# Sums of w_down beside the output projection, moving tiles on GpSimd's queue, and later products with ones, in a hybrid SSD and ConvFFN decoder step

## The chip, the cores and the metric

The kernel runs on one core of a Trainium2 chip. The metric is the device time of one execution in microseconds (us), lower is better. Before the change three runs gave 1511.21, 1513.53 and 1514.72 us, with a median of 1513.53.

The engines are named as in the profile: PE is the matrix engine (TensorE) and PEld its loading of weights, DVE is VectorE, ACT is ScalarE, POOL is GpSimd. SP is SyncE, which here only starts transfers. Transfers can be started by SP, ACT and POOL; each starts its own in the order in which the program puts them, and an instruction that waits holds back all that stands behind it on the same engine.

## The reference

One layer of a decoder is computed for 1032 tokens (a prompt of 1024 and 8 single-token samples), all in float32:

```python
x = x + jnp.concatenate([y_ssd, y_pool], axis=-1) @ w_out      # 2048 -> 1024
hn = rmsnorm(x, norm2_w)
u = hn @ w_up                                                  # 1024 -> 2 x 2816
u, ffn_new = causal_dwconv(u, ffn_buf, ffn_conv_w, ffn_conv_b)
gate, val = jnp.split(u, 2, axis=-1)
x = x + (jax.nn.silu(gate) * val) @ w_down                     # 2816 -> 1024
y = rmsnorm(x, final_norm_w)
```

What comes before it (input projection, short convolution, chunked SSD scan, windowed means) gives `y_ssd` and `y_pool`; the change doesn't touch it.

## The kernel before, in words

Everything is held with channels on the 128 partitions and the 1032 tokens along the free dimension. To keep the accuracy of float32, each operand of a matmul is split into a high part, rounded by ACT (L137 for weights, L207 for moving tiles), and a low part, the difference made by DVE (L138, L208). Each product of two tiles is then three matmuls (high x high, high x low, low x high).

**Output projection** (`w_out`, L834). It runs in three parts over the contraction, 6, 6 and 4 tiles of 128. In each of the first two parts a loop goes over the 8 output tiles n: `load_tile` loads the weights `wout` in two pieces on SP's queue (L127, into four buffers called `raw`), 54 matmuls of 344 columns are made (L156 to L158), and DVE adds the result to the residual `x2[n]` (L855). The third part (`w_out_end`, L877) runs by halves of the tokens, stores x2 to DRAM as `x2d` (L893, SP), makes the squares for the RMSNorm and scales x2 by it (L915).

**Up-projection** (`up_pair`, L1013, 22 pairs). `w_up` and `w_down` are multiplied by Strassen's scheme in Winograd's form: seven products p1 to p7 of half-sized blocks in place of eight. `moving` (L925) makes the sums of blocks of the normalised x2 and their splits, once; these are the moving operands of all 22 pairs. `up_weights` (L975) makes the sums of blocks of the weights by accumulating transfers: SP loads a block into a buffer `s` (L985), and GpSimd's queue adds another to it during a transfer (L987). The chain is p5 from two blocks, p6 from one block plus p5, p3 from one plus p6, and p7 from two. Each product of a pair is 24 matmuls of 258 columns (`blocks`, L990, matmul L1008), 168 in a pair. Behind a pair come the convolution (L1053, L1055), SiLU and the product with the value (L1065); every second pair `spill` (L1079) makes the block sums of the activations and ACT's queue stores them to DRAM as `td`.

**Sums of w_down** (`down_sums`, L1095). The down projection's seven products need four sums of blocks of `w_down` (p5, p7, p6, p3). The contraction is cut in three pieces s (`PIECES`: 4, 4 and 3 tiles), and the output in four column pairs m. For each of the twelve (m, s), SP loads four blocks `ds` (L1104), GpSimd makes four additions (`mix`, L1107) and GpSimd's queue stores each result to DRAM as `sd` (L1109). `phase_ffn` (L1310) calls it once behind each pair from the third on (L1326); the blocks lie in five buffers of the pool `sums`, where the seven buffers `s` lie as well.

**Down projection** (`down`, L1159). The products come in the order p1, p2, p5, p6, p7, p4, p3. `down_ops` (L1117) loads the 11 moving tiles of a product from `td` (L1124, SP's queue) and splits them; `down_weights` (L1131) loads a piece of weights, from `w_down` or from `sd` (L1142, SP's queue); `piece` (L1145) makes 12 or 9 matmuls (L1154), so that a product is 264. `sink` adds the results to the residual, which `load_x2` (L1167) brings back from `x2d` in front of p2; the additions that read only SBUF are GpSimd's (L1182), those that read PSUM are DVE's. `square` (L1208) collects squares for the last RMSNorm, added by GpSimd (L1216).

**Last block.** p3 runs by quarters q of the tokens, and in each over the four column pairs. Beside its matmuls stand products with ones, which sum squares over the partitions: of `ssq[1]` ahead of the first column pair (L1259), and of the pair's own squares behind each pair (L1272). After the first column pair `norm_half` (L1294) makes the norm of the first half of the tokens: two products with ones (L1301), eight multiplications on DVE (L1305) and eight stores of `yT` on SP's queue (L1308). At the end of each quarter the norm is applied (L1280, L1288) and stored (L1286, L1292).

A scheduler orders the instructions of each engine when the program is built, by its own estimate of times and by the buffers; it doesn't keep the order of the source. `issue_after` (`behind`, L172) is the means to force one instruction behind another.

## Time and profile before

| | |
|---|---|
| median of three runs | 1513.53 us |
| the profiled execution | 1515.61 us, of which its span 1513.8 us |
| mean granted clock of PE | 0.961 |
| output projection, matmuls of the first two parts | about 556 to 692 us of the span |
| up-projection, first to last matmul | 747.7 to 1243.1 us |
| down projection, first to last matmul | 1250.2 to 1504.9 us |
| moved by transfers | 227.53 MB, 150 GB/s on average |

The profile is that of one execution. Its page gives the busy time of each engine, the share that each line has in the chain of work that ended last, and groups of instructions by line. The trace behind it can also be asked for stretches of time, for the waits between engines (who waited for whom, total, times, longest), and for the order of events on one engine. A busy time of PE counts each matmul from start to end; matmuls overlap, so the pace is read from a count of matmuls in a stretch.

### The profile page before, as it was taken

The numbers are of one execution on the slowest core, as the hardware profiler recorded it, in microseconds if no ns is written. First come the engines' busy times: TensorE is split into PE (matmuls) and PEld (weight loads), VectorE is DVE, ScalarE is ACT, GpSimd is POOL, SyncE is SP. The second block draws the span as 40 slices with busy tenths as digits, with TensorE's granted clock in tenths as the row PEclk, the third lists the DMA queues.
The fourth block names the chain that finished last, engine by engine and source line by source line (L and its number), as shares of the span: only waits on it lengthen the run. The fifth ranks groups of instructions, "written<-read, shape, count | busy, mean of one in ns | idle before, by whom it ended". The sixth has DMA issues, their size and how long they took to land.

```text
span 1513.8 us, 26445 instructions
## 1 busy us (share of the span) xinstructions
PE 1411.6 (93%) x10312; PEld 1334.4 (88%) x10312; DVE 998.7 (66%) x1442; ACT 669.8 (44%) x1220; POOL 542.0 (36%) x536
## 2 busy tenths in 40 slices
PE   8999999798999999999839989999999989999977
PEld 6889878776699999999839989999999989999966
DVE  6484786699953482524778978877777765667532
ACT  6246443255245451313435444545555554454422
POOL 5153677768621100001386766322222101003310
PEclk9999999999899999999959999999999999999989
DMA  6031333333311142124559999977777766765431
GB/s 231 8 94 56 110 118 115 121 109 126 110 46 37 46 149 66 47 56 135 180 146 251 306 295 273 265 191 184 195 182 189 186 204 231 246 222 184 133 113 57
DMA packets 132120, 227.53 MB, mean 150 GB/s; under 512 B 27852, under 2 KB 45084, under 8 KB 131996
## 3 DMA queue, kind: packets, MB, share of 16 engines
q1 hardware_dynamic: 102012, 170.31, 35.3%
q0 software_dynamic: 16256, 34.61, 11.3%
q10 hardware_dynamic: 13728, 20.93, 4.2%
q8 instruction: 81, 1.33, 0.4%
q14 instruction: 43, 0.35, 0.1%
HBM read 169.11 MB, written 45.15 MB: 142 GB/s over the span
## 4 chain that ended last, share of the span: by engine, by line
PE 68%; DMA 10%; DVE 10%; POOL 6%; issue 4%; ACT 2%; SPq 1%; DVEq 0%; ACTq 0%; POOLq 0%
PE g L1008 22%; PE g L1154 10%; PE g L157 10%; PE g L156 10%; PE g L158 10%; DMA g<-td 3%; DVE wop L138 2%; POOL ds L1107 2%; DMA s<-wup 2%; PE pY L579 2%; PE pY L583 1%; DMA ds<-wdn 1%; DMA mix<-acd 1%; PE pT L534 1%; PE pT L532 1%
## 5 line engine op out<-in xcount | busy, mean ns | idle before, releaser
L1008 PE MATMUL g<-op,wop 128*128 128x258 f32 x3696 | 454.1, 286 | 41.4 <-ACT wop L137 23.0
L1008 PEld LDWEIGHTS g<-op,wop 128*128 128x128 f32 x3696 | 451.2, 192 | 44.2 <-ACT wop L137 33.0
L1154 PE MATMUL g<-op,wop 128*128 128x258 f32 x1848 | 233.6, 288 | 12.9 <-ACT op L207 8.4
L1154 PEld LDWEIGHTS g<-op,wop 128*128 128x128 f32 x1848 | 228.9, 193 | 17.2 <-ACT op L207 9.4
L156 PE MATMUL g<-hh,wop 128*128 128x344 f32 x696 | 229.1, 329 | 2.9 <-ACT u L464 2.8
L138 DVE TENSOR_TENSOR wop<-raw,wop 128x512 fp32r<-128x512 f32 (+1 forms) x186 | 142.9, 774 | 130.1 <-ACT wop L137 129.3
L158 PE MATMUL g<-hh,wop 128*128 128x344 f32 x696 | 227.1, 326 | 0.0
L157 PE MATMUL g<-hl,wop 128*128 128x344 f32 x696 | 226.5, 325 | 0.0
L137 ACT ACTIVATE wop<-raw 128x512 fp32r<-128x512 f32 (+1 forms) x208 | 125.5, 607 | 227.8 <-PE g L158 137.2
L156 PEld LDWEIGHTS g<-hh,wop 128*128 128x128 f32 x696 | 134.0, 193 | 4.7 <-ACT u L464 3.5
L158 PEld LDWEIGHTS g<-hh,wop 128*128 128x128 f32 x696 | 133.7, 192 | 1.2 <-issue 1.1
L157 PEld LDWEIGHTS g<-hl,wop 128*128 128x128 f32 x696 | 134.0, 193 | 0.5 <-issue 0.5
L1055 DVE SCALAR_TENSOR_TENSOR acc<-u,cst,acc 128x1048 f32<-128x1048 f32 x88 | 124.5, 1415 | 10.7 <-ACT acc L1053 9.3
L137 ACT ACTIVATE wop<-s 128x512 fp32r<-128x512 f32 (+1 forms) x136 | 82.4, 614 | 97.2 <-PE g L1008 39.1
L138 DVE TENSOR_TENSOR wop<-s,wop 128x512 fp32r<-128x512 f32 (+1 forms) x136 | 105.7, 783 | 29.0 <-ACT wop L137 28.1
L987 POOL DMA_DIRECT2D s<-s x44 | 40.0, 909 | 200.5 <-DMA s<-wup 88.6
L1040 ACT ACTIVATE u<-g 128x258 f32<-128x258 f32 (+2 forms) x220 | 69.1, 338 | 77.4 <-PE g L1008 66.1
L1107 POOL TENSOR_TENSOR ds<-ds,ds 128x512 f32<-128x512 f32 (+1 forms) x48 | 87.6, 1835 | 28.4 <-DMA ds<-wdn 28.1
L1043 DVE TENSOR_TENSOR u<-u,g 128x258 f32<-128x258 f32 (+2 forms) x176 | 57.4, 352 | 58.7 <-PE g L1008 57.1
L479 DVE SCALAR_TENSOR_TENSOR xs<-u,cst,xs 128x1056 f32<-128x1056 f32 x48 | 78.3, 1647 | 23.9 <-ACT xs L477 23.6
L158 PE MATMUL g<-yh,wop 128*128 128x344 f32 x288 | 91.8, 320 | 0.0
L157 PE MATMUL g<-yl,wop 128*128 128x344 f32 x288 | 91.8, 320 | 0.0
(262 smaller groups left out, 2313.9 us busy)
## 6 DMA issues: line engine op xcount, KB each, us to landing
s<-wup SPq DMA_DIRECT2D x88, 256.0 KB, 4.7
g<-td SPq DMA_DIRECT2D x77, 258.0 KB, 3.7
raw<-wup SPq DMA_DIRECT2D x66, 256.0 KB, 5.0
raw<-win SPq DMA_DIRECT2D x58, 256.0 KB, 2.6
mix<-acd SPq DMA_DIRECT2D x16, 768.0 KB, 6.0
td<-acc ACTq DMA_DIRECT2D x22, 516.0 KB, 5.7
s<-wup POOLq DMA_DIRECT2D x44, 256.0 KB, 6.1
s<-s POOLq DMA_DIRECT2D x44, 256.0 KB, 4.6
```

What stands on the lines that cost most here:

```text
L137: self.nc.scalar.activation(hi, raw[:, :w], AF.Copy)
L138: lo_eng.tensor_tensor(out=lo, in0=raw[:, :w], in1=hi.bitcast(F32), op=ALU.subtract)
L156: nc.tensor.matmul(ps[:, :n], wh, xh[:, sl], start=(first and k == 0), stop=False)
L157: nc.tensor.matmul(ps[:, :n], wh, xl[:, sl], start=False, stop=False)
L158: nc.tensor.matmul(ps[:, :n], wl, xh[:, sl], start=False, stop=(final and k == last))
L479: nc.vector.scalar_tensor_tensor(out=out, in0=u[:, k : k + SW], scalar=self.c("cw", 4 * ct + k), in1=out, op0=ALU.mult, op1=ALU.add)
L1008: nc.tensor.matmul(out, a, b, start=(p in OPENS and j == 1), stop=(j == 12), skip_group_check=True)
L1040: a = nc.scalar.activation(out, ps[:, s], AF.Copy, scale=-1.0 if p in ("p5", "p4") else 1.0)
L1043: nc.vector.tensor_tensor(out=out, in0=out, in1=ps[:, s], op=op)
L1055: nc.vector.scalar_tensor_tensor(out=acc, in0=u[:, k : k + FW], scalar=self.c("fw", 3 * n + k), in1=acc, op0=ALU.mult, op1=ALU.add)
L1107: nc.gpsimd.tensor_tensor(out=out, in0=in0, in1=in1, op=op)
L1154: nc.tensor.matmul(out, a, b, start=(s == 0 and i == 0 and j == 0), stop=(s == len(PIECES) - 1 and i == nk - 1 and j == 2),)
```

## The change

Four things are edited.

1. `down_sums` is called in the output projection, once at each output tile of the first two parts until the twelve are done. Its blocks take buffers that the pooling groups leave behind (`v`, `mh`, `ml`, `sa`, `sb`, 4 KB a partition each), two sets by turns, and the five buffers `ds` are gone.
2. The loads of moving tiles (`td`), the loads of `x2d` and the stores of `norm_half` are started by GpSimd in place of SP. The loads of `x2d` come behind the tiles of p1.
3. The 32 additions of `sink` that read only SBUF go from GpSimd to DVE, and squares get two buffers of their own in place of buffers `s`.
4. In the last block the products with ones wait for one column pair more, by a list `held` and by `behind`; `norm_half` follows the second column pair.

```diff
+        self.sums = {}
+        todo = [(m, s) for s in range(len(PIECES)) for m in range(KT // 2)]
...
             for n in range(KT):
+                if todo:
+                    self.down_sums(len(todo), *todo.pop(0))
...
-    def down_sums(self, m, s):
+    def down_sums(self, i, m, s):
...
+        mk = lambda tag, bufs=1: self.ph.tile([P, 2, 512], F32, tag=tag, name=self.nm("ds"), bufs=bufs)
+        x, y, z = mk("v", 2), mk(("mh", "ml")[i % 2]), mk(("sa", "sb")[i % 2])
+        blk = {"11": x[:, 0, :w], "12": x[:, 1, :w], "21": y[:, 0, :w], "22": y[:, 1, :w]}
...
-                self.nc.sync.dma_start(st[:, j], self.td[i + j][ROW[p]])
+                self.loaded = self.nc.gpsimd.dma_start(st[:, j], self.td[i + j][ROW[p]]).ins
...
-                nc.sync.dma_start(t, self.x2d[n])
+                with self.behind(self.loaded):
+                    nc.gpsimd.dma_start(t, self.x2d[n])
...
-                add(nc.gpsimd, block(0, 0), u)
+                add(nc.vector, block(0, 0), u)
...
-        mksq = lambda: self.raw(True)
+        mksq = lambda: self.ph.tile([P, TH], F32, tag="sq", name=self.nm("sq"), bufs=2)
...
-            if p == "p2":
+            if p == "p1":
                 load_x2()
...
-            nc.tensor.matmul(pb[:, :TQ], self.ones, ssq[1][:, part], start=True, stop=False)
+            held = [ssq[1][:, part]]
+
+            def ones(stop=False):
+
+                with self.behind(self.pe):
+                    nc.tensor.matmul(pb[:, :TQ], self.ones, held.pop(0), start=(m == 1), stop=stop)
...
-                nc.tensor.matmul(pb[:, :TQ], self.ones, sq, start=False, stop=(m == NM - 1))
-                if q == 0 and m == 0:
-                    self.norm_half(x2, 0, ssq[0], r_of(0))
+                held.append(sq)
+                if m:
+                    ones()
+                if q == 0 and m == 1:
+                    with self.behind(self.pe):
+                        self.norm_half(x2, 0, ssq[0], r_of(0))
+            ones()
+            ones(True)
...
-            nc.sync.dma_start(d["yT"][:, n, cols], x)
+            nc.gpsimd.dma_start(d["yT"][:, n, cols], x)
...
-                    if j >= 2 and todo:
-                        self.down_sums(*todo.pop(0))
```

The built programs show what the scheduler makes of it. First GpSimd at the opening of the up-projection. A row has the line, the operation and what it writes and reads: `s` are sums of up weights, `wup` their blocks, `ds` and `sd` the sums of w_down, `u` the tiles of the convolution. Before:

```order
L987 DMA s_6955<-wup 128x512
L987 DMA s_6963<-wup 128x512
L987 DMA s_7209<-wup 128x512
L987 DMA s_6958<-s_6955 128x512
L987 DMA s_7217<-wup 128x512
L1107 TENSOR_TENSOR ds_7718<-ds_7716,ds_7718 128x512
L1109 DMA sd_7726<-ds_7718 128x512
L1107 TENSOR_TENSOR ds_7716<-ds_7720,ds_7716 128x512
L1107 TENSOR_TENSOR ds_7724<-ds_7718,ds_7720 128x512
L987 DMA s_7212<-s_7209 128x512
L1109 DMA sd_7729<-ds_7716 128x512
L987 DMA s_6966<-s_6958 128x512
```

With the change (its L992 is L987 of before):

```order
L992 DMA s_7183<-wup 128x512
L992 DMA s_7191<-wup 128x512
L992 DMA s_7437<-wup 128x512
L992 DMA s_7186<-s_7183 128x512
L992 DMA s_7445<-wup 128x512
L992 DMA s_7440<-s_7437 128x512
L992 DMA s_7194<-s_7186 128x512
L1026 MEMSET u_7175 128x2
L1027 COPY u_7175<-fst_7173 128x24
```

The load of p3's sum (`s_6966` before, `s_7194` now) stood behind three additions and two stores of `down_sums`, and now stands behind other accumulating loads alone.

Second, SP in the first two parts of the output projection. Before, weights follow weights:

```order
L127 DMA raw_5393<-wout 128x384
L127 DMA raw_5398<-wout 128x384
L127 DMA raw_5463<-wout 128x384
L127 DMA raw_5468<-wout 128x384
L127 DMA raw_5533<-wout 128x384
```

With the change (`ds` are blocks of w_down, x2 marks two equal rows):

```order
L127 DMA raw_5596<-wout 128x384
L127 DMA raw_5601<-wout 128x384
L1110 DMA ds_5222<-wdn 128x512 x2
L127 DMA raw_5685<-wout 128x384
L127 DMA raw_5690<-wout 128x384
L1110 DMA ds_5221<-wdn 128x512 x2
L1110 DMA ds_5311<-wdn 128x512 x2
L127 DMA raw_5798<-wout 128x384
L127 DMA raw_5803<-wout 128x384
```

`ds_5222` and `ds_5221` belong to the third sum and take the buffers of the first; the weights behind them wait on the queue until the first sum's additions and stores have let those buffers go.

Third, SP at the last block. Before (`s` from `sd` are weights of p3, `yT` from `x` the stores of `norm_half`):

```order
L1142 DMA s_15377<-sd_7735 128x512
L1142 DMA s_15394<-sd_8853 128x512
L1142 DMA s_15411<-sd_9971 128x384
L1308 DMA yT<-x_13330 128x516
...
L1308 DMA yT<-x_13344 128x516
L1142 DMA s_15455<-sd_8015 128x512
L1142 DMA s_15472<-sd_9133 128x512
```

With the change (`raw` from `wdn` are weights of p4, the product before):

```order
L1148 DMA s_15352<-sd_5060 128x512
L1148 DMA s_15369<-sd_5416 128x512
L1148 DMA s_15386<-sd_5796 128x384
L1148 DMA s_15405<-sd_5149 128x512
L1148 DMA s_15422<-sd_5505 128x512
L1148 DMA s_15439<-sd_5885 128x384
L1148 DMA s_15483<-sd_5238 128x512
L1148 DMA raw_15046<-wdn 128x512
L1148 DMA raw_15075<-wdn 128x384
L1148 DMA raw_15110<-wdn 128x512
L1148 DMA raw_15139<-wdn 128x512
```

The stores of `norm_half` are off this queue, and seven of the twelve weights of p3 (the `s` of these rows) stand ahead of the last weights of p4.

More of the change, by code (lines that the diff above doesn't have):

```diff
@@ L1099, in down_sums @@
         w = nk * P
-        blk = {}
-        for k, i, e in (("21", 1, 0), ("22", 1, 1), ("11", 0, 0), ("12", 0, 1)):
-            blk[k] = self.spool.tile([P, 512], F32, tag="ds", name=self.nm("ds"), bufs=5)[:, :w]
+        mk = lambda tag, bufs=1: self.ph.tile([P, 2, 512], F32, tag=tag, name=self.nm("ds"), bufs=bufs)
+        x, y, z = mk("v", 2), mk(("mh", "ml")[i % 2]), mk(("sa", "sb")[i % 2])
+        blk = {"11": x[:, 0, :w], "12": x[:, 1, :w], "21": y[:, 0, :w], "22": y[:, 1, :w]}
+        for k, r, e in (("21", 1, 0), ("22", 1, 1), ("11", 0, 0), ("12", 0, 1)):
             o = (e * DK + k0) * P
-            nc.sync.dma_start(blk[k], d["wdn"][2 * m + i][:, o : o + w])
+            nc.sync.dma_start(blk[k], d["wdn"][2 * m + r][:, o : o + w])
         def mix(p, out, in0, in1, op):
@@ L1109, in mix @@
             nc.gpsimd.dma_start(self.sums[p, m, s], out)
-        s2 = self.spool.tile([P, 512], F32, tag="ds", name=self.nm("ds"), bufs=5)[:, :w]
+        s2 = z[:, 0, :w]
         mix("p5", blk["22"], blk["21"], blk["22"], ALU.add)
@@ L1153, in piece @@
             for j, (a, b) in enumerate(((wh, xh), (wh, xl), (wl, xh))):
-                nc.tensor.matmul(
+                self.pe = nc.tensor.matmul(
                     out, a, b, start=(s == 0 and i == 0 and j == 0),
                     stop=(s == len(PIECES) - 1 and i == nk - 1 and j == 2),
-                )
+                ).ins
     def down(self):
@@ L1193, in sink @@
                 add(nc.vector, u, ps)
-                add(nc.gpsimd, block(0, 1), u)
+                add(nc.vector, block(0, 1), u)
             elif p == "p7":
                 add(nc.vector, u, ps)
-                add(nc.gpsimd, block(1, 1), u)
+                add(nc.vector, block(1, 1), u)
             elif p == "p4":
-                add(nc.gpsimd, block(1, 0), u)
+                add(nc.vector, block(1, 0), u)
                 add(nc.vector, block(1, 0), ps)
@@ L1223, in down @@
                 ops = self.down_ops(p)
-            if p == "p2":
+            if p == "p1":
                 load_x2()
-            if p == "p1":
                 ps = [[self.gps() for _ in range(2)] for _ in range(NM)]
@@ L1321, in phase_ffn @@
                 self.x2 = None
-                self.td, self.puts, self.sums = [], [], {}
-                todo = [(m, s) for s in range(len(PIECES)) for m in range(half)]
+                self.td, self.puts = [], []
                 for j in range(FT):
                     self.up_pair(j, ops, FIRST if j in (0, FT - 1) else ORDER)
-                    if j >= 2 and todo:
-                        self.down_sums(*todo.pop(0))
                 self.put(None)
```

## The prediction

> **What bounds the kernel now.** I read the busy line of the page first, then a table of the stages from the output projection to the end, then the waits of the matrix engine, and then the chain and the queues inside the stages that lose time.
>
> ```profile
> PE 1411.6 (93%) x10312; PEld 1334.4 (88%) x10312; DVE 998.7 (66%) x1442; ACT 669.8 (44%) x1220; POOL 542.0 (36%) x536
> ```
>
> PE is busy for 93% of the span, so the kernel is bound by matmuls, and a change can win only where PE waits or runs at a low clock. The stage table shows where that is. Its columns are: stretch and length; then busy time and instructions of PE, PEld, DVE, ACT and POOL; granted PE clock; DMA share; GB/s. The last line is one product with ones, two passes, from the chain of waits.
>
> ```profile
> 747.70:802.00 54.30, 26.01 (x163) 24.67 (x162) 40.52 (x58) 22.05 (x42) 41.01 (x30) 0.69 0.66 175
> 802.00:940.00 138.00, 124.87 (x1006) 123.48 (x1005) 117.63 (x137) 60.42 (x131) 93.92 (x117) 0.96 0.97 287
> 940.00:1243.00 303.00, 303.00 (x2532) 303.00 (x2532) 226.01 (x350) 158.86 (x335) 71.53 (x126) 1.00 0.76 198
> 1243.00:1250.20 7.20, 0.27 (x3) 0.06 (x2) 3.11 (x3) 5.09 (x7) 0.00 (x0) 0.67 1.02 386
> 1250.20:1447.60 197.40, 194.63 (x1584) 192.62 (x1584) 118.76 (x199) 91.28 (x166) 37.56 (x40) 0.99 0.60 192
> 1447.60:1504.90 57.30, 44.02 (x289) 40.27 (x288) 20.43 (x32) 17.29 (x38) 4.65 (x3) 0.88 0.28 94
> 1504.90:1513.80 8.90, 0.00 (x0) 0.00 (x0) 2.96 (x3) 0.89 (x2) 1.69 (x1) 0.69 0.34 119
> ```
>
> ```profile
> 1498.13 0.44 PE g L1272 x2
> ```
>
> The third row is the yardstick: 2532 matmuls in 303.0 us, 0.1197 us each, at full clock. The up-projection has 3696 matmuls; the 1164 before 940 are worth 139.3 us and took 192.3, so **53.0 us are lost in its opening**. Between 1243.0 and 1250.2 PE stands still, and the 1584 matmuls of the six following products take 197.4 us where 189.6 would do: **15.0 us lost at the start of the down projection and in it**. The last product (264 matmuls, 31.6 us, and 24 passes of products with ones at some 0.22 us, 5.2) takes 57.3 us: **20.5 us lost in the last block**. The final 8.9 us have no matmul and stay.
>
> **Part one: the sums leave the up-projection.** The chain of waits says what the opening waits for (start, length, what):
>
> ```profile
> 758.02 1.21 POOL s L987
> 759.23 17.81 POOL ds L1107
> ...
> 780.40 0.91 POOL s L987
> 781.57 6.22 DMA s<-s
> 787.81 1.67 ACT wop L137 x3
> ```
>
> One addition of `down_sums` (L1107) stood on GpSimd for 17.8 us, and the accumulating load of the weights of p3 (L987) was queued behind it until 780.40. It landed at 787.8, and PE idled for 16.3 us in one piece:
>
> ```profile
> PE g L1008 <- ACT wop L137: 23.0, 3, 16.3
> PE g L1154 <- ACT op L207: 8.4, 2, 6.9
> PE g L1259 <- POOL ssq L1216: 4.3, 1, 4.3
> ```
>
> The change takes all 48 additions, 48 loads and 48 stores out of here. What is late next is DVE, which makes the moving operands of the first pair without a pause from 749.29:
>
> ```profile
> 749.29 5.42 DVE L915 SCALAR_TENSOR_TENSOR x<-x,cst,rh 128x516 f32<-128x516 f32 x8 [4.01 <-ACT rh L185]
> 776.50 5.14 DVE L208 TENSOR_TENSOR op<-x,op 128x516 fp32r<-128x516 f32 x3
> 770.38 4.94 DVE L208 TENSOR_TENSOR op<-x,op 128x516 fp32r<-128x516 f32 x8
> ```
>
> Eight splits in 4.94 us are 0.62 each, so the last three need 1.9 us when GpSimd isn't in the way, and DVE ends at about 778.4 instead of 781.6. With p4's 24 matmuls (2.9 us) after it, the first pair is done by about 782. In those 34.3 us PE has then issued the pair's 168 matmuls and, by its order, some 24 of the next: 23.0 us of work, so about 11 are lost, and I add 5 for matmuls at the low clock (0.69 in the first row): 16 kept. From 802 to 940 the lost 17.6 us go with the transfers: the DMA share is 0.97 there and 0.76 in the row after it, which is the same loop without sums. I keep 2. Gain: 53.0 - 18 = **35 us** (43 if only 10 are kept; 19 if the later stalls stay).
>
> **Part two: the sums beside the output projection.** This stage has no idle PE to give. Its room is read from the stretch 556 to 692 (same columns) and from two splits of weights that are one tile of output apart, 8.50 us. The last line is the product of the pooling groups, whose tiles the sums reuse:
>
> ```profile
> 556.00:692.00 136.00, 136.00 (x865) 136.00 (x864) 57.21 (x94) 30.94 (x49) 1.61 (x1) 1.00 0.27 82
> 580.98 0.53 ACT L137 ACTIVATE wop<-raw 128x384 fp32r<-128x384 f32 x1 [6.55 <-PE g L158]
> 589.48 0.53 ACT L137 ACTIVATE wop<-raw 128x384 fp32r<-128x384 f32 x1 [6.55 <-PE g L158]
> L158 PE MATMUL pY<-mh,pw x4: 319/319/323, 538.1 to 567.9; 128*128 128x344 f32 x4
> ```
>
> GpSimd is idle, DVE 42% busy, the DMA share 0.27. One sum costs GpSimd four additions and four stores; the nearest rows are the same ones from 802 on:
>
> ```profile
> L1107 POOL TENSOR_TENSOR ds<-ds,ds 128x512 f32<-128x512 f32 x25 | 40.3, 1612 | 17.7 <-DMA ds<-wdn 17.5
> L1109 POOL DMA_DIRECT2D sd<-ds x40 | 29.3, 759 | 3.6 <-POOL ds L1107 3.6
> ```
>
> That is 4 x 1.61 + 4 x 0.76 = 9.5 us a sum, twelve sums in about 110 us, from about 578 (the tiles come free at 567.9, and some 10 us go for weights ahead on the queue and for the first loads) to 690. The danger is the sync queue: the loads of a sum wait there for GpSimd's stores of the sum two before, and the `wout` loads stand behind them. In the new order the weights of the first tile of the third part stand behind sum 10's first blocks, which need sum 8 nearly finished. With p for a sum, 578 + 8.75p + 11.6 (landing of the store, load, split) must be under 692.4, so p under 11.7. At 9.5 nothing is late. I charge **2 us**, for the first sums and for DVE's splits that meet an addition (bounds 0 and 15).
>
> **Part three: moving tiles on GpSimd's queue.** Today 77 loads of `td` share the sync queue with the weights and with x2d; the first is issued behind four x2d loads that wait for the last pair's operands.
>
> ```profile
> 1243.14 1.19 SPq L1124 DMA_DIRECT2D g<-td  x2
> ```
>
>  So it cannot land before 1246. In the changed order GpSimd has nothing else left, the eleven first tiles stand before x2d, and the first of them waits only for p1 of the last pair, some 17 us before the up-projection ends (a pair of 20.1 less p1's 2.9). So the 7.2 us gap closes but for about 1. Later products have their tiles free while the product before them runs, 31.6 us earlier, so a slower queue is hidden by a whole product; I keep 2 of the 7.8. On that queue the third x2d load waits for the last matmuls of the up-projection, with p2's tiles behind it (needed 31.6 us later), and three additions of squares (L1216) stand among p7's tiles, a product ahead of need. Gain **12 us** (14 to 4). The prices behind it (issue on GpSimd, landing by either queue, from the groups of DMAs from 980 to 1200 and of the page):
>
> ```profile
> L987 POOL DMA_DIRECT2D s<-wup x22 | 23.3, 1061 | 5.3 <-DVE u L1043 2.8 <-DVE acc L1055 1.2 <-DMA s<-wup 1.0
> s<-wup POOLq DMA_DIRECT2D x22, 256.0 KB, 5.7
> g<-td SPq DMA_DIRECT2D x77, 258.0 KB, 3.7
> ```
>
> 85 loads at 1.06 us are 90 us of GpSimd in about 220, and 2.0 us more to land. The 32 additions that go to DVE cost at most the price of a PSUM addition there, 32 x 0.42 = 13 us, beside 118.8 busy of 197.4: not on the path.
>
> ```profile
> L1182 DVE TENSOR_TENSOR x<-x,g 128x258 f32<-128x258 f32 x31 | 11.9, 418 | 10.9 <-PE g L1154 7.7 <-POOL x L1182 3.2
> ```
>
> The Trainium skill speaks against this part: "SBUF — State Buffer", section "SBUF: two separate sides", says that descriptors of GpSimd's DMAs cannot be written while VectorE holds the shared port, and advises the SP or ACT queue. The 1.06 us per issue under a DVE that is 75% busy is all that these rows show of it; the rival below prices it.
>
> **Part four: the last block.** The chain there:
>
> ```profile
> 1450.19 1.73 POOL ssq L1216
> 1451.96 1.23 PE g L1259 x2
> ...
> 1456.34 5.42 DVE x L1305 x8
> 1461.76 0.35 DVE x L1182
> ...
> 1462.21 2.95 DMA s<-sd
> 1465.19 0.64 ACT wop L137
> ```
>
> PE's order has a product with ones on `ssq` at the front, so it waits for GpSimd (4.3 us); the norm of the first half sits on DVE ahead of the sum of column pair 0; and nine weight loads stand on the sync queue behind eight stores that need that norm (the first store waited until 1457.12, the first load until 1462.21).
>
> ```profile
> 1457.12 5.00 SPq L1308 DMA_DIRECT2D yT<-x  x8
> 1462.21 12.21 SPq L1142 DMA_DIRECT2D s<-sd  x9
> ```
>
> All three go: the ones follow the second column pair, the stores go to GpSimd's queue (behind them wait only GpSimd's two last multiplications, L1280, the first of them off the path and the second some 15 us later), seven of p3's twelve weight tiles are requested before most of p4's, and the squares no longer take buffers of the weights. What is late next: ACT's order still has the square of pair 0 ahead of the splits for pair 1, so PE waits once for add, square and split, about 2.0 us; the last square costs 1 as before. I keep 4.5: gain **16 us** (18 to 10).
>
> **Sum.** 35 - 2 + 12 + 16 = 61 us. The profiled execution took 1515.6 (span 1513.8 and 1.8 around it), 2.1 above the median 1513.5; the gain is taken from the median: 1452.5, rounded to **1453 us**, 4.0% faster. A measurement of this kernel can tell about 0.2%, 3 us, from no change.
>
> **The rivals.** (A) *The opening stays slow.* DVE ran at 85% from 802 to 940, above the 75% of the rows after, and each pair's accumulating loads form a chain of transfers; if that and not the sums is the limit, the 15.6 us that I let go there stay: 1469. For it: the stretch follows 30 us in which weights are hardly used. Against: nothing in the loop differs from that after 940 but the sums. 0.12. (B) *GpSimd's queue is late.* If the issue is held up by DVE so that lookahead is lost, each of six products starts with the extra landing and issue of its first tile, 2.0 + 1.06 us: 6 x 3.1 = 18, and 1471. For it: the row of 1.06 us. Against: a product of 31.6 us as cover. 0.10. By the skill's rule above it is this case that comes. (C) *Slower.* The output projection starves: additions there meet DVE's splits, p passes 11.7, and from then each further microsecond costs about 8.75 of PE, since every weight load queues behind a sum. At p = 18.7 the whole gain is gone. If every sum had one addition like the 17.8 us one, p would be 17.8 + 3 x 1.61 + 4 x 0.76 = 25.7, the loss 8.75 x 14.0 = 122, and the time 1453 + 122 - 2 = 1573. For it: that one addition, under a DVE that never paused. Against: DVE is 42% busy here. 0.04, and 0.02 for losses that about cancel the gain. The Trainium skill, same section, has the port as an exclusive lock held for the whole instruction; that is the mechanism of C, and 48 additions at 1.6 us beside 57 us of DVE fit into 136.
>
> **How the numbers follow.** My case has 0.72, over 1438 (bounds 43, 14 and 18, and 0 lost) to 1468; A and B add 0.22 up to 1471, and both together give 1487. I take 1438 to 1485. All but C and the cancelling case are faster: 0.94 faster, 0.02 same, 0.04 slower.
>
> **What would show it.** Right: no GpSimd addition of `down_sums` after the output projection, PE at full clock there, a wait of PE of a few us at most after the first pair, the up-projection ending near 1210 and the last product taking about 41 us. Wrong: PE waiting on splits of `wout` weights between 600 and 720 (C), a DMA share near 1 and idle PE after the first pair (A), or PE waiting on ACT's operand splits at each product's start, behind `td` loads (B).

## The result, and the profile after

Four runs of the changed kernel gave 1466.6 to 1474.5 us, median 1471.4; four of the kernel before gave 1504.5 to 1514.7, median 1512.4. The ratio is 0.9735 with a 95% interval of 0.969 to 0.978: faster by 2.7%, 41 us, where 61 were forecast. The profiled execution has a span of 1470.6 us, 43.2 less than before.

The busy line of the page after:

```profile
PE 1401.2 (95%) x10312; PEld 1327.4 (90%) x10312; DVE 982.2 (67%) x1474; ACT 668.0 (45%) x1220; POOL 552.6 (38%) x597
```

The stages after, with the columns of the prediction's table (stretch and length; busy time and instructions of PE, PEld, DVE, ACT, POOL; granted PE clock; DMA share; GB/s):

```profile
554.60:696.70 142.10, 139.06 (x874) 138.68 (x873) 72.53 (x96) 31.50 (x50) 89.18 (x97) 0.99 0.72 238
751.50:802.00 50.50, 34.60 (x229) 33.36 (x228) 39.14 (x65) 26.17 (x51) 22.61 (x21) 0.80 0.65 147
802.00:940.00 138.00, 138.00 (x1153) 138.00 (x1153) 102.56 (x160) 72.87 (x155) 31.19 (x56) 1.00 0.76 188
940.00:1217.90 277.90, 277.90 (x2319) 277.90 (x2319) 204.00 (x320) 143.22 (x303) 60.49 (x109) 1.00 0.75 196
1217.90:1222.30 4.40, 0.31 (x4) 0.10 (x2) 1.26 (x2) 4.37 (x7) 2.27 (x5) 1.00 0.58 155
1222.30:1285.00 62.70, 59.61 (x456) 58.69 (x457) 36.79 (x63) 26.87 (x53) 14.52 (x27) 0.92 0.70 250
1285.00:1420.20 135.20, 135.20 (x1133) 135.20 (x1132) 92.96 (x173) 64.42 (x117) 34.59 (x52) 1.00 0.56 178
1420.20:1461.70 41.50, 39.15 (x289) 37.36 (x287) 16.89 (x29) 15.47 (x35) 8.10 (x11) 0.96 0.25 88
1461.70:1470.60 8.90, 0.00 (x0) 0.00 (x0) 2.96 (x3) 0.89 (x2) 1.69 (x1) 0.71 0.35 119
```

From 802 on the up-projection is PE alone, at full clock, with a DMA share of 0.76: the 17.6 us that were lost between 802 and 940 are gone. What it still loses lies in its first 50.5 us, where 229 matmuls run that are worth 27.4. In the down projection all losses lie ahead of 1285. Set side by side, with stages bounded by the first and last matmul (the last product starts 33 matmuls before 1424.2, at about 1420.2):

| stage | before, us | after, us | gain | forecast |
|---|---|---|---|---|
| ahead of the output projection's first two parts | 554.2 | 553.2 | 1.0 | 0 |
| first two parts of the output projection | 138.5 | 143.3 | -4.8 | -2 |
| third part and norm | 55.0 | 55.0 | 0 | 0 |
| up-projection | 495.3 | 466.4 | 28.9 | 35 |
| its end to the last product | 204.6 | 202.3 | 2.3 | 12 |
| last product | 57.3 | 41.5 | 15.8 | 16 |
| after it | 8.9 | 8.9 | 0 | 0 |
| sum | 1513.8 | 1470.6 | 43.2 | 61 |

The waits of PE that remain, longest in total first (engine, line, waited for; total, times, longest):

```profile
PE g L1013 <- ACT wop L137: 5.8, 1, 5.8
PE g L1160 <- ACT op L207: 5.6, 2, 4.1
...
PE g L1013 <- ACT u L1045: 5.3, 3, 2.5
PE g L1013 <- DVE wop L138: 4.9, 1, 4.9
...
PE g L157 <- DVE yl L208: 3.0, 1, 3.0
```

Before, the first of these was 23.0 us with one piece of 16.3. Three of them are of use below: 3.0 for a moving tile in the output projection, 5.3 for ACT's `u` in the opening, 5.6 at products' starts in the down projection. The 5.8 and the 4.9 lie in the opening too, and stood there before the change with the same lengths.

**Output projection.** The groups of DVE between 560 and 700, each form apart (total, mean ns | idle before). Before:

```profile
L855 DVE TENSOR_TENSOR x<-x,g 128x344 f32<-128x344 f32 x48 | 24.4, 511 | 54.3 <-PE g L158 54.2
L138 DVE TENSOR_TENSOR wop<-raw,wop 128x384 fp32r<-128x384 f32 x28 | 15.6, 557 | 17.9 <-ACT wop L137 17.3
L208 DVE TENSOR_TENSOR yl<-xs,yh 128x1032 fp32r<-128x1032 f32 x6 | 7.3, 1231 | 0.2
```

After:

```profile
L860 DVE TENSOR_TENSOR x<-x,g 128x344 f32<-128x344 f32 x48 | 24.3, 510 | 46.3 <-PE g L158 46.3
L138 DVE TENSOR_TENSOR wop<-raw,wop 128x384 fp32r<-128x384 f32 x28 | 23.2, 827 | 16.5 <-ACT wop L137 14.6 <-DMA ds<-wdn 1.5
L208 DVE TENSOR_TENSOR yl<-xs,yh 128x1032 fp32r<-128x1032 f32 x6 | 12.4, 2097 | 0.2
```

The same splits, with both operands in SBUF, take 827 in place of 557 ns and 2097 in place of 1231. The additions of `x<-x,g`, whose second operand is in PSUM, take 510 as before. On DVE's own timeline the low parts for the next part come in a burst in which it never pauses (start, length):

```profile
616.71 9.01 DVE L208 TENSOR_TENSOR yl<-xs,yh 128x1032 fp32r<-128x1032 f32 x4
...
627.20 2.30 DVE L208 TENSOR_TENSOR yl<-xs,yh 128x1032 fp32r<-128x1032 f32 x1
```

Four splits need 9.01 us there, and the fifth is the one that PE waits 3.0 us for. Each of these five took 2.1 to 2.5 us, where one alone takes 1.23: it lasts about an addition of GpSimd (1.3 us) longer.

**Opening of the up-projection.** GpSimd's timeline there:

```profile
771.34 9.66 POOL L1027 COPY u<-fst 128x24 f32<-128x24 f32 x1
780.95 0.86 POOL L992 DMA_DIRECT2D s<-s  x1
...
781.53 1.34 POOL L1027 COPY u<-fst 128x24 f32<-128x24 f32 x1
```

And what ACT waits for there:

```profile
782.90 0.18 ACT L1045 ACTIVATE u<-g 128x8 f32<-128x8 f32 x1 [5.38 <-POOL u L1027]
```

A copy of 24 columns, for which 40 such copies from 802 to 1217 took 0.81 us on average, stands for 9.66 us. It is of the same kind as the 17.8 us addition of before, at the same place: DVE makes moving tiles here without a pause, until 780.85, when it comes to an addition that reads PSUM. Behind the copy on GpSimd stand an accumulating load (of p3's weights of the second pair, by the order of the program) and the copy for the other `u` tile. ACT waits 5.38 us for that second copy, and PE for ACT: it is the copy itself that is missed, not the load.

**Start of the down projection.** ACT, DVE, GpSimd and PE, in order of time:

```profile
1217.26 1.08 ACT L185 ACTIVATE acc<-acc 128x1048 f32<-128x1048 f32 x1
1218.36 1.28 ACT L178 ACT_TABLE_LOAD   x1
...
1220.45 1.25 ACT L1058 ACTIVATE acc<-u,cst 128x1048 f32<-128x1048 f32 x1
...
1221.60 1.15 ACT L207 ACTIVATE op<-g 128x516 fp32r<-128x516 f32 x2
1221.73 2.65 DVE L1060 SCALAR_TENSOR_TENSOR acc<-u,cst,acc 128x1048 f32<-128x1048 f32 x2 [0.46 <-ACT acc L1058]
...
1222.28 1.49 PE L1160 MATMUL g<-op,wop 128*128 128x258 f32 x8 [4.09 <-ACT op L207]
1224.31 0.69 DVE L208 TENSOR_TENSOR op<-g,op 128x516 fp32r<-128x516 f32 x1
```

The first moving tiles were requested from 1200 on, as forecast, but their split (L207) stands on ACT behind the SiLU of the last pair, a table load, a split of weights and a convolution. The low part (L208) stands on DVE behind two more steps of the convolution. ACT has no gap between these rows and DVE one of 0.46 us: it is their order, not a transfer.

### The profile page after: what moved, and what is told of

It is laid out like the page before. It is cut to its first block, busy times and chain, and to the rows that moved or that the text cites. A ratio compares the mean times of both kernels' runs of the same rounds, so it can differ in the third digit from the quotient of the medians.

```text
span 1470.6 us, 26434 instructions
## 1 busy us (share of the span) xinstructions
PE 1401.2 (95%) x10312; PEld 1327.4 (90%) x10312; DVE 982.2 (67%) x1474; ACT 668.0 (45%) x1220; POOL 552.6 (38%) x597
## 4 chain that ended last, share of the span: by engine, by line
PE 82%; DVE 7%; POOL 4%; DMA 3%; issue 2%; ACT 2%; SPq 0%; DVEq 0%; POOLq 0%; ACTq 0%
PE g L1013 29%; PE g L1160 15%; PE g L157 10%; PE g L158 10%; PE g L156 10%; PE pY L579 2%; PE pY L583 1%; DMA mix<-acd 1%; PE pT L534 1%; DMA st<-st_ssm 1%; PE pT L532 1%; POOL st L622 1%; POOL st L623 1%; DVE x L292 1%; PE pM L557 1%
## 5 line engine op out<-in xcount | busy, mean ns | idle before, releaser
L1013 PE MATMUL g<-op,wop 128*128 128x258 f32 x3696 | 450.8, 285 | 15.9 <-ACT wop L137 5.8
L1013 PEld LDWEIGHTS g<-op,wop 128*128 128x128 f32 x3696 | 449.3, 191 | 17.2 <-ACT u L1045 6.0
L992 POOL DMA_DIRECT2D s<-s x44 | 38.6, 878 | 286.0 <-DMA s<-wup 84.2
L1060 DVE SCALAR_TENSOR_TENSOR acc<-u,cst,acc 128x1048 f32<-128x1048 f32 x88 | 115.2, 1309 | 12.1 <-ACT acc L1058 10.6
L138 DVE TENSOR_TENSOR wop<-s,wop 128x512 fp32r<-128x512 f32 (+1 forms) x136 | 91.2, 677 | 37.1 <-ACT wop L137 35.0
L479 DVE SCALAR_TENSOR_TENSOR xs<-u,cst,xs 128x1056 f32<-128x1056 f32 x48 | 83.5, 1756 | 22.0 <-ACT xs L477 21.7
L1130 POOL DMA_DIRECT2D g<-td x77 | 41.9, 548 | 143.7 <-DVE op L208 68.1
```

Source lines behind the costliest of these rows:

```text
L138: lo_eng.tensor_tensor(out=lo, in0=raw[:, :w], in1=hi.bitcast(F32), op=ALU.subtract)
L479: nc.vector.scalar_tensor_tensor(out=out, in0=u[:, k : k + SW], scalar=self.c("cw", 4 * ct + k), in1=out, op0=ALU.mult, op1=ALU.add)
L1013: nc.tensor.matmul(out, a, b, start=(p in OPENS and j == 1), stop=(j == 12), skip_group_check=True)
L1060: nc.vector.scalar_tensor_tensor(out=acc, in0=u[:, k : k + FW], scalar=self.c("fw", 3 * n + k), in1=acc, op0=ALU.mult, op1=ALU.add)
L1130: self.loaded = self.nc.gpsimd.dma_start(st[:, j], self.td[i + j][ROW[p]]).ins
```

## The experiments

All ratios are to the kernel before, run on the same chip beside them, with 95% intervals. Stages are bounded by first and last matmuls, as in the table.

**The sums alone.** The kernel before with the first of the four edits:

```diff
+                if todo:
+                    self.down_sums(len(todo), *todo.pop(0))
...
-                    if j >= 2 and todo:
-                        self.down_sums(*todo.pop(0))
```

> Only the sums of w_down are moved beside the output projection; queues, additions of the down projection and the last block are as before. The sum of the prediction has 35 - 2 = 33 us for this part, so 1479 us from 1512. The stages of the changed kernel's profile (output projection 4.8 us longer, up-projection 466.4 in place of 495.3 us) say 28.9 - 4.8 = 24, so 1488. Rival: the parts are not additive, and the opening of the up-projection was gained by something else of the change as well: then less than 15 us, above 1497. In the profile: full clock and no idle PE from 802 on by both of the first two.

Measured: 1487.1 us, ratio 0.983 (0.979 to 0.986). First two parts of the output projection 143.5, up-projection 466.1, and the pause at the start of the down projection 7.8. So this edit has its whole gain and its whole loss alone; the size is the one of the profile after, not that of the prediction.

**The queues alone.** The kernel before with moving tiles and x2d on GpSimd's queue and all additions of the down projection on DVE:

```diff
-                self.nc.sync.dma_start(st[:, j], self.td[i + j][ROW[p]])
+                self.loaded = self.nc.gpsimd.dma_start(st[:, j], self.td[i + j][ROW[p]]).ins
...
-                add(nc.gpsimd, block(0, 0), u)
+                add(nc.vector, block(0, 0), u)
```

> Only the moving tiles and x2d go to GpSimd's queue, and the additions of the down projection to DVE; the sums stay in the up-projection. The prediction has 12 us for this, 1500 from 1512. By the profile after, the pause of PE ahead of the first product is set by ACT and DVE, which still have the convolution and SiLU of the last pair in front of the first split, and what it leaves behind is a lowered clock: then 2 to 3 us, 1509. Rival B: GpSimd's queue is late at each of six products, 18 us slower, 1530; here with the sums' additions out of the way in the down projection, so nothing hides it.

Measured: 1511.4 us, ratio 1.0005 (0.998 to 1.003). In its profile the pause shrinks from 7.2 to 4.4 us, and the wait that is left is again that for ACT:

```profile
PE g L1154 <- ACT op L207: 5.6, 2, 4.1
```

The row is, to the tenth, that of the changed kernel. The forecast of 12 us for this part is refuted, and so is rival B: nothing is slower either. (The 2.8 us by which the pause is shorter are too few for this interval to show.) The loads' own rows, of the changed kernel, say why:

```profile
L1130 POOL DMA_DIRECT2D g<-td x77 | 41.9, 548 | 143.7 <-DVE op L208 68.1 <-PE g L1160 38.0 <-DMA td<-acc 13.4
```

An issue took 548 ns on average, half of the 1061 that I had taken from the accumulating loads, and it is GpSimd that waits, for splits and matmuls to let buffers go. The section of the Trainium skill that the prediction named ("SBUF — State Buffer", "SBUF: two separate sides") lets DVE keep GpSimd from writing descriptors while it runs an instruction in a two-port performance mode. These 77 loads, issued while DVE was 59 to 69% busy, took between 546 and 577 ns each, so it doesn't show here; whether any of DVE's instructions ran in such a mode, no trace says.

**The last block undone.** The changed kernel with its last block as before:

```diff
-                held.append(sq)
-                if m:
-                    ones()
...
+                nc.tensor.matmul(pb[:, :TQ], self.ones, sq, start=False, stop=(m == NM - 1))
+                if q == 0 and m == 0:
+                    self.norm_half(x2, 0, ssq[0], r_of(0))
...
-            nc.gpsimd.dma_start(d["yT"][:, n, cols], x)
+            nc.sync.dma_start(d["yT"][:, n, cols], x)
```

> The changed kernel with the last block as before: ones ahead, norm of the first half behind the first column pair, its stores on SP's queue, squares in the weights' buffers. Prediction and profile agree on 16 us for this part: 1471 + 16 = 1487. Rival: with the moving tiles off SP's queue and the additions on DVE, the weights of the last block are early anyway, and the gain belongs to part three: then below 1477.

Measured: 1489.3 us, ratio 0.983 (0.979 to 0.987), 18 more than the changed kernel's median. That compares two sets of runs; in the profile the last product takes 56.2 us in place of 41.5, so 14.7 of its 15.8 us come back. The gain belongs to the last block, as forecast; the rival falls.

**Each addition three times.**

```diff
+            for _ in range(2):
+                nc.gpsimd.tensor_tensor(out=z[:, 1, :w], in0=in0, in1=in1, op=op)
             nc.gpsimd.tensor_tensor(out=out, in0=in0, in1=in1, op=op)
```

> The changed kernel with each addition of the sums made three times, two of them into a scratch tile; the result is unchanged. With the profile's 1.31 us per addition and 0.56 per store, a sum takes 12 x 1.31 + 4 x 0.56 = 18.0 us of GpSimd in place of 7.5. Rival C of the prediction (weights queue behind the sums, from 11.7 us on each further microsecond of p costs 8.75): 6.3 x 8.75 = 55 us slower than the changed kernel, 1526, with PE waiting for splits of output weights from about 600 on. If the cost lies in DVE's splits that meet additions alone: the 4.8 us of the output projection become at most 15, 1481. If the queue has room that the formula leaves out: no change, 1471.

Measured: 1558.9 us, ratio 1.031 (1.025 to 1.036): 88 more than the changed kernel and slower than before. Rival C's side was right, its place wrong. The first two parts take 155.4 us, 12.1 more, with these waits:

```profile
PE g L157 <- DVE yl L208: 9.4, 1, 9.4
...
PE g L158 <- DVE wop L138: 2.7, 1, 2.7
```

None of them is weights that come late behind a sum on SP's queue. The 9.4 us are one split:

```profile
624.19 11.10 DVE L208 TENSOR_TENSOR yl<-xs,yh 128x1032 fp32r<-128x1032 f32 x1
```

It stood while GpSimd made seven additions with hardly a gap; the four splits ahead of it took 1.2 to 2.3 us. The bulk, 70.6 us, stands behind the third part, ahead of the norm:

```profile
PE pT L908 <- ACT sq L903: 60.5, 1, 60.5
ACT ssq L900 <- DMA sd<-ds: 49.4, 1, 49.4
```

The squares of the third part take the buffers of the sums, and ACT waits 49.4 us for the store of one (L900 is the first square). The last addition of the sums starts at 808.9, where it started at 692.1 in the changed kernel; there the last store is issued at 693.5 and the first square made at 700.2. So in the changed kernel the sums were done some 7 us ahead of the first instruction that takes their buffers. How much of that is margin isn't shown exactly: with three additions the first square ran at 800.3, ahead of the last addition, so it needs the buffers of an earlier sum. The contention also grows with the additions (DVE between 560 and 780):

```profile
L138 DVE TENSOR_TENSOR wop<-raw,wop 128x384 fp32r<-128x384 f32 x28 | 54.0, 1928 | 12.2 <-ACT wop L137 12.1
L208 DVE TENSOR_TENSOR yl<-xs,yh 128x1032 fp32r<-128x1032 f32 x5 | 17.0, 3411 | 0.1
```

These means (1928 and 3411 ns) are not a common factor: the second is the split of 11.10 us with four of 1.2 to 2.3, and in the first a few splits of 4 to 11.5 us stand beside others of 0.5 to 2.3.

**No additions.** The changed kernel, where each store takes a block as it was loaded:

```diff
-            nc.gpsimd.tensor_tensor(out=out, in0=in0, in1=in1, op=op)
...
-            nc.gpsimd.dma_start(self.sums[p, m, s], out)
+            nc.gpsimd.dma_start(self.sums[p, m, s], in0)
```

> The changed kernel without the additions of the sums: the loads and stores stay, and each store takes an unsummed block (so the down projection gets other weights). Beside the additions DVE's splits took 2.27 us in place of 1.23 (moving tiles) and 0.85 in place of 0.56 (weights), and PE waited 3.0 us for one of them. If the additions alone do that, the output projection's two parts go from 141.9 us back to 137 and the time to 1467. If the 24 MB more of transfers do it, the splits of weights wait on loads as now, PE's wait stays and the time is 1471.

Measured: 1466.5 us, ratio 0.967 (0.964 to 0.971). The first two parts take 138.5 us, as before the change (the expectation counts the two states as 141.9 and 137 us, the table's bounds as 143.3 and 138.5); the wait of 3.0 us is gone. The transfers alone cost nothing.

**The additions on DVE.**

```diff
+                if making:
+                    making.pop(0)()
                 if todo:
-                    self.down_sums(len(todo), *todo.pop(0))
+                    making.append(self.down_sums(len(todo), *todo.pop(0)))
...
-            nc.gpsimd.tensor_tensor(out=out, in0=in0, in1=in1, op=op)
+            nc.vector.tensor_tensor(out=out, in0=in0, in1=in1, op=op)
```

> The changed kernel with the 48 additions of the sums on DVE, each sum one output tile later, so that its blocks have landed; the stores stay on GpSimd's queue. 48 additions at 0.55 to 0.7 us are 30 us more on DVE, which is busy for 57 us of 137 without contention. If the contention of the two engines is the whole cost of the sums, the output projection goes from 141.9 us to 137 to 139: 1468. Rival: DVE now waits for blocks in its own order, the splits of weights behind them are late and PE starves: above 1476.

Measured: 1468.9 us, ratio 0.970 (0.968 to 0.973); the first two parts take 138.6. DVE's groups from 574 to 694:

```profile
L1110 DVE TENSOR_TENSOR ds<-ds,ds 128x512 f32<-128x512 f32 x24 | 15.8, 686 | 1.7 <-DMA ds<-wdn 1.7
L138 DVE TENSOR_TENSOR wop<-raw,wop 128x384 fp32r<-128x384 f32 x26 | 14.4, 555 | 9.9 <-ACT wop L137 9.7
...
L208 DVE TENSOR_TENSOR yl<-xs,yh 128x1032 fp32r<-128x1032 f32 x5 | 6.1, 1228 | 0.0
```

The splits are back at 555 and 1228 ns with all the additions made. With the run before this settles the 4.8 us: not the work, nor the transfers, but two engines at work on SBUF at once. The Trainium skill ("SBUF — State Buffer", "SBUF: two separate sides") has a port that GpSimd and DVE share as a lock, taken by a DVE instruction with two SBUF inputs against a GpSimd instruction that reads SBUF; that the additions with a PSUM operand kept their 510 ns agrees with it.

**The first pair's copy on ACT.**

```diff
+            if j == 0:
+                nc.scalar.activation(u[:, 0:2], fst[:, i, 0:2], AF.Copy, scale=0.0)
+                nc.scalar.activation(u[:, 1026:FUW], fst[:, i, :], AF.Copy)
+            else:
-            nc.gpsimd.memset(u[:, 0:2], 0.0)
-            nc.gpsimd.tensor_copy(u[:, 1026:FUW], fst[:, i, :])
+                nc.gpsimd.memset(u[:, 0:2], 0.0)
+                nc.gpsimd.tensor_copy(u[:, 1026:FUW], fst[:, i, :])
```

> The changed kernel with GpSimd's memset and copy of 24 state columns (L1026, L1027) of the first pair made by ACT. In the changed kernel this copy stood on GpSimd for 9.66 us, from 771.3 to 781.0, while DVE worked without a pause; the accumulating load of p3's weights was queued behind it, and ACT waited 5.4 us for it. If a GpSimd instruction that touches SBUF waits for a pause of DVE, as the 17.8 us addition did before the change, the copy's wait goes, the accumulating load is issued at about 772, and the opening loses 5 to 8 us less: 1465. Rival, by the Trainium skill (SBUF — State Buffer, SBUF: two separate sides), by which the descriptors of GpSimd's DMAs are locked out in the same way: the load itself then stands there until 781 and the time stays 1471. Second rival: DVE's splits end at 782 anyway and bind alone: 1470.

Measured: 1461.6 us, ratio 0.967 (0.964 to 0.969). The up-projection takes 460.5 us, 5.9 less. GpSimd's row of the accumulating load there:

```profile
768.99 0.87 POOL L992 DMA_DIRECT2D s<-s  x1 [6.71 <-DVE wop L138]
```

PE's timeline has no stop left from 772.37 to 802, the end of the stretch asked for:

```profile
772.37 29.88 PE L1013 MATMUL g<-op,wop 128*128 128x258 f32 x234 [2.18 <-ACT u L1049]
```

The rival by the Trainium skill falls: the load at 768.99 was issued in 0.87 us in the middle of the burst, in which DVE worked without a pause from 759.72 to 777. What DVE held up was the copy, not the descriptors, and what ACT had waited for was the copy, not the load, as ACT's row under "Opening of the up-projection" has it. The second rival, that DVE's splits bind alone, falls too. The time is 9 us below the changed kernel's, more than this stage gives: the first two parts of the output projection took 140.4 us in this profile and the down projection 2.5 less, though nothing was edited in either. Of the five splits that met additions in the changed kernel, two took 1.2 us here and not 2.3, so that loss varies from one program to the next; what sets it is open.

**Four tiles earlier.** The changed kernel, where the last pair calls for the first four tiles of the down projection ahead of its convolution:

```diff
         self.blocks(self.up_weights(j), ops, sink, order)
+        if j == FT - 1:
+            self.early = self.down_ops("p1", 0, 4)
...
-        ops = self.down_ops("p1")
+        ops = self.early + self.down_ops("p1", 4)
```

> The changed kernel with the first four moving tiles of the down projection loaded and split ahead of the convolution of the last pair in the order of the program. In the changed kernel these tiles had landed while ACT had SiLU, a table load, a weight split and a convolution in front of their first split, and DVE two steps of the convolution; PE paused 4.1 and 1.3 us and then ran at a lower clock. If the order on ACT and DVE sets the pause, it goes for about 5 us and up to 3 of the clock: 1464 to 1466. Rival, the sum of the prediction, in which the loads' queue sets it: no change, 1471, with PE waiting for tiles five to eleven instead.

Measured: 1464.7 us, ratio 0.969 (0.966 to 0.972). Up- and down-projection together take 701.9 us, 6.3 less. PE's timeline:

```profile
1220.34 1.61 PE L1162 MATMUL g<-op,wop 128*128 128x258 f32 x12
1221.79 1.61 PE L1013 MATMUL g<-op,wop 128*128 128x258 f32 x12
...
1225.29 29.67 PE L1162 MATMUL g<-op,wop 128*128 128x258 f32 x247
1257.18 0.75 PE L1162 MATMUL g<-op,wop 128*128 128x258 f32 x4 [2.23 <-ACT op L207]
```

The matmuls of both projections (L1013 and L1162) interleave and the pause is gone, with the loads on the same queue as in the changed kernel. At the start of p2 it is longer instead: 2.23 us and 0.74 in place of 1.51 and 0.24.

**x2d later.** The changed kernel with four of the eight loads of x2d behind the tiles of p2:

```diff
-                load_x2()
+                load_x2((0, 2, 4, 6))
...
+            if p == "p2":
+                load_x2((1, 3, 5, 7))
```

> The changed kernel with four of the eight loads of x2d (the odd tiles, needed first in p5) behind the moving tiles of p2. In the changed kernel the DMA share is 1.0 from 1222 to 1254, and p2's first tile, requested at 1249.3, was split only at 1258.9, for which PE waited 1.5 us and ran at a lower clock to 1285. If the transfers of x2d hold that tile up, 2 to 3 us are won: 1469. If it is the buffers (p2's tiles get theirs when p1's matmuls let go of them), the wait stays and the time is 1471.

Measured: 1467.8 us, ratio 0.971 (0.969 to 0.974), beside 1470.5 and 0.973 (0.971 to 0.975) for the changed kernel in the same round. PE's timeline at p2's start:

```profile
1262.58 5.75 PE L1160 MATMUL g<-op,wop 128*128 128x258 f32 x46 [0.23 <-DVE op L208]
1269.09 6.37 PE L1160 MATMUL g<-op,wop 128*128 128x258 f32 x48 [0.77 <-ACT op L207]
```

In the changed kernel one pause of 1.51 us stood there; 0.23 and 0.77 are left. But the 2.7 us of the time are within the intervals, and the down projection is 2.5 us shorter in the run with the copy on ACT as well, where nothing in it was edited. What these loads cost, beyond half a microsecond of pauses, stays open.

**Three and four together.**

> The changed kernel with the last three edits together: state columns of the first pair on ACT, additions of the sums on DVE, the first four moving tiles ahead of the last pair's convolution. If the three losses are separate, the stages add: output projection 138.6 (4.7 less), up-projection 459 to 460 (5.9 and a little less), up- and down-projection together 6.4 less: 17 us, 1471 - 17 = 1454, which is near what the prediction said of the change. If the first two share a cause that either removes, or the work that goes to ACT and DVE comes back as a wait, 1458 or more.

Measured: 1451.0 us, ratio 0.960 (0.958 to 0.963), 19.5 less than the changed kernel of the same round (1470.5). First two parts of the output projection 139.0 us, up- and down-projection together 693.0 in place of 708.2. Its stages from 800 to 1270:

```profile
800.00:1204.60 404.60, 404.60 (x3382) 404.60 (x3381) 299.67 (x469) 213.19 (x447) 93.60 (x163) 1.00 0.76 195
1204.60:1270.00 65.40, 62.57 (x515) 61.70 (x515) 40.45 (x71) 33.09 (x62) 17.86 (x33) 1.00 0.75 270
```

PE's clock is full across the change of projections, where it was 0.92 over 62.7 us. The three losses add up (17 us expected, 19.5 measured), so they are separate, and this version beats both kernels.

> All four edits together. If each loss is separate: 1454 less 2 to 3, 1451. If the loads of x2d cost nothing: as the three, 1454.

Measured with x2d later too: 1454.9 us, ratio 0.962 (0.959 to 0.964). Nothing is added to the three.

> The changed kernel itself once more, as the yardstick for the three others: 1471 by all theories.

Measured: 1470.5 us, ratio 0.973 (0.971 to 0.975).

## Why the prediction came out as it did

The direction, the stages and the order of the gains were right, and the time fell in the range; the size was 18 us too good. My own case ended at 1468, 3 us short of the measured time; the range reached far enough by rivals A and B, at 1469 and 1471. Neither of them came about: A wanted the stretch to 940 to stay slow, and it runs at full clock; B wanted GpSimd's queue late. That the time is theirs is chance, and three other terms of the sum make it.

1. **Opening, 35 forecast, 28.9 measured.** "I keep 2" for the stretch from 802 to 940 was right (0). The step that was mis-sized is "16 kept" in the first pair: 24 stayed. I had named DVE as what is late next, and its run took 29.7 us where the forecast had 29.1. But I had assumed GpSimd out of the way: edit 1 took the additions from its queue and left the state copies there, which ran into the same burst, and ACT and PE waited for them. With the copy on ACT the stage is 5.9 us shorter, and 24 becomes 18. (One reading was off by 1.2 us, and nothing hangs on it: the load issued at 780.40 before the change is p6's of the second pair, and p3's of the first left at 781.57.)
2. **Output projection, -2 forecast, -4.8 measured**, inside the bounds of 0 and 15. The mechanism was named ("DVE's splits that meet an addition") and its price too low: that five splits in a row would take 2.1 to 2.5 us each in place of 1.2 was not looked for. Without additions, or with the additions on DVE, nothing is lost. The 9.5 us for a sum were good: the twelve took 120 us from first addition to last store, 10.0 each with their waits for loads.
3. **Down projection, 12 forecast, 2.3 measured**, below the bound of 4. This is the step that failed: "So the 7.2 us gap closes but for about 1" was worked out from the queue of the loads alone. The tiles came early as said, and their splits did not, since ACT and DVE had the last pair's convolution ahead. In the trace of before the same SiLU, table load and convolution ran inside the 7.2 us; I gave the whole gap to the loads because a load ended last there, and 4.4 us of it stayed. "I keep 2 of the 7.8" failed as well, since 8.3 stayed: this loss isn't spread over the products but lies in the first 63 us, in pauses of 3.1 us (1.28, 1.51, 0.24) and in the clock of 0.92 (62.7 x 0.08 = 5.0), of which the queue changes nothing. Tiles split earlier gave 6.3 us of it.
4. **Last block, 16 forecast, 15.8 measured**, and 14.7 in its stage by undoing it. Each of its waits was where the chain had it.

Rival C is shown to exist, since three additions in place of one make the kernel slower than before. The point from which it decides was not at p = 11.7 by weights behind sums, but where the squares of the third part take the sums' buffers, some 7 us behind the last store of the changed kernel.

What stays open: about 18 us in the first pair of the up-projection, while DVE makes the moving tiles; 1.5 to 3 us at the start of p2; how near the sums are to costing time; and the 2.5 us by which the down projection differs between kernels that don't touch it.

## What to carry to other kernels

When a wait is taken away, walk the same queue of each engine up to the waiting instruction and ask what else stands there: the gap of 7.2 us was ended by a load and had 4.4 us of ACT and DVE right under it. When work moves from one engine's crowded stretch to another's quiet one, price it by what it does to the neighbour that shares its memory, not only by its own time: the additions fitted into idle GpSimd, and it was DVE that paid. And when a small instruction of a slow engine can be held up by a long run of a fast one, take all such instructions out of that stretch, not only the large ones.

## What the runs showed of the hardware

- A GpSimd copy of 24 columns stood 9.66 us, and before the change an addition 17.8 us, under an unbroken run of DVE instructions on SBUF; they ended at 781.00 and 777.04, right behind DVE's first instructions with a PSUM operand (from 780.85 and from 775.83). It is not one DVE instruction (0.6 us) that is waited for but the whole run. That DVE holds it is inferred from the place and from the copy that is gone; what in the hardware does it wasn't tried.
- The same went in the other direction. Beside GpSimd's additions of 1.3 us, DVE's splits took 827 in place of 557 ns and 2097 in place of 1231 on average; and with each addition made three times, one split of 1.23 us stood 11.10 us under seven additions in a row. DVE's additions from PSUM kept 504 to 510 ns in both runs. So a mean hides what happens: most splits take their usual time or up to about one addition more, and a few wait out a run of additions.
- Starting a transfer on GpSimd was not held up: an accumulating load between two tiles in SBUF took 0.87 us inside DVE's unbroken run, which is also its mean from 802 to 1217, and a moving tile 0.55 us with DVE 59 to 69% busy.
- Nor was one GpSimd instruction that only writes: in the same burst a memset of two columns took 0.10 us at 771.30, right ahead of the copy that stood 9.66.
